# Weight sums for the seven-product down units: built in device memory by copying and adding DMAs

## The chip, the cores and the metric

The kernel runs on one core of a Trainium2 chip. The metric is the device time of one execution in microseconds. All arithmetic on the data is float32, and a matrix product is made of three products of split operands (a rounded part "hi" and a remainder "lo", in a reduced float32 form that TensorE takes).

## The reference

A two-layer decoder trunk on a sequence of 512 tokens, width 1024. Each layer has a token mixer (attention heads), an MLP with a squared ReLU, and a gated embedding:

```python
for i in range(DEPTH):                                   # DEPTH = 2
    hn = rmsnorm(h, norm_mix_g[i])
    h = h + mixer(hn, ...)                               # even: stick-breaking + differential; odd: dilated
    hn = rmsnorm(h, norm_mlp_g[i])
    u = jnp.square(jax.nn.relu(hn @ w_mlp_up[i]))        # 1024 -> 4096
    h = h + u @ w_mlp_down[i]                            # 4096 -> 1024
    gate = jax.nn.sigmoid(rmsnorm(h, norm_ple_g[i]) @ w_ple_gate[i])
    h = h + (p[i] @ w_ple_proj[i]) * gate
return rmsnorm(h, final_norm_g)
```

The change concerns `u @ w_mlp_down[i]` alone.

## The kernel before, in words

The layers run one after the other: mixer, MLP, gated embedding. Weights lie in device memory, packed into blocks of 1 MiB ([128 partitions, 2048 columns]). `wload` fetches one block into a tile called `raw`, of which there are two buffers; `wsplit` makes `wh` (ScalarE, line 122) and `wl` (GpSimd, line 126, in two halves, inside the mixers; VectorE, line 128, elsewhere) of half a block at a time, each with three buffers, and TensorE then runs the three products (lines 141, 144, 145). The DMA that loads `raw` (line 114) is issued from SyncE's queue; that queue also carries the attention bias tiles (`bias<-urow`, line 543), the stores of the embedding's projection (`pjd`, line 384) and everything else that is a plain copy. DMAs that add into their target are issued from GpSimd's queue, where the `wl` subtractions of the mixers also stand. Each queue is worked in order: a DMA or an instruction that waits holds back what stands behind it on the same queue. The order in which each engine's instructions stand is made by a scheduling layer when the kernel is built. It may put an instruction ahead of ones written earlier in the code, as long as what it depends on is kept. A DMA is told finished through one of eight semaphores that the queue's DMAs use in turn, so at most eight from SyncE's queue are under way.

The MLP runs in four chunks of 1024 hidden columns. `up(ch, c)` makes a quarter of a chunk's hidden values; `down(ch, c)` multiplies a chunk by one of four column groups of the down weights. A `down` unit is a 2 by 2 block product done with seven block products instead of eight (a Winograd scheme): its 1 MiB block of weights holds four quarters A12, A22, A21, A11, and besides the quarters it needs four sums of them,

- S1 = A21 + A22 and S3 = A21 + A11 (tile `s13`),
- S2 = S1 + A11 and S4 = S2 + A12 (tile `s24`).

In chunks 0 to 2 VectorE makes the four sums with four additions of [128, 512] (lines 799, 800, 801, 804). In chunk 3 `s13` is made by two loading DMAs on SyncE's queue (line 783) and one adding DMA on GpSimd's (line 784), and VectorE makes only `s24`. The sixteenth unit of a layer (chunk 3, group 3) is computed in the plain way and needs no sums. So 15 units in each of two layers use sums. `split` (line 813 on ScalarE, 814 on VectorE) then makes the hi and lo tiles.

Of the kernel before, what the change touches and what calls it, by code (L numbers as in the profile page):

```python
# [12 lines left out]
F32 = mybir.dt.float32  # L13
# [3 lines left out]
ALU = mybir.AluOpType  # L17
AX = mybir.AxisListType

P = 128  # L20
D = 1024
S = 512
# [5 lines left out]
DEPTH = 2  # L28
# [34 lines left out]
def trunk(  # L63
# [5 lines left out]
    nc = tc.nc  # L69
    uid = [0]  # L70

    def nm(s):
        uid[0] += 1
        return f"{s}_{uid[0]}"

    cpool = ctx.enter_context(tc.tile_pool(name="cpool", bufs=1))
    dpool = ctx.enter_context(tc.tile_pool(name="dpool", bufs=1, space=bass.MemoryType.DRAM))
# [26 lines left out]
    def ps_wide():  # L104
        t = ps(wide[wide_i[0] % 8])
        wide_i[0] += 1
        return t
# [4 lines left out]
    def wload(src):  # L112
        raw = wpool.tile([P, src.shape[-1]], F32, tag="raw", name=nm("raw"), bufs=2)
        nc.sync.dma_start(raw, src)
        return raw

    def wsplit(raw, i, nk, n, pool=None):
        bufs = 3 if pool is None else 4
        hi = (pool or wpool).tile([P, nk, n], F32R, tag="wh", name=nm("wh"), bufs=bufs)
        lo = (pool or wpool).tile([P, nk, n], F32R, tag="wl", name=nm("wl"), bufs=bufs)  # L120
        src = raw[:, i * nk * n:(i + 1) * nk * n].rearrange("p (k c) -> p k c", k=nk)
        act = nc.scalar.activation(hi, src, AF.Copy)  # L122
        if lo_eng[0] is nc.gpsimd:
            for x in range(2):
                kx = slice(x * nk // 2, (x + 1) * nk // 2)
                nc.gpsimd.tensor_tensor(lo[:, kx], src[:, kx], hi[:, kx].bitcast(F32), op=ALU.subtract)  # L126
        else:
            last_low[:] = [nc.vector.tensor_tensor(lo, src, hi.bitcast(F32), op=ALU.subtract).ins]  # L128
        last_high[:] = [act.ins]
        return hi, lo  # L130
# [3 lines left out]
    def block(src, nk, n):  # L134
        raw = wload(src)
        return [wsplit(raw, i, nk, n) for i in range(src.shape[-1] // (nk * n))]
# [15 lines left out]
    def lin_units(accs, ws, ahl, k0, nk, outer):  # L152
        pairs = [(i, k) for k in range(nk) for i in range(len(accs))] if outer else \
            [(i, k) for i in range(len(accs)) for k in range(nk)]
        for i, k in pairs:
            ah, al = ahl[k0 + k]
            mm3(accs[i], ws[i][0][:, k], ws[i][1][:, k], ah, al, k == 0, k == nk - 1)
            yield 2.0

    def run(units):  # L160
        for _ in units:
            pass
# [62 lines left out]
    def use_tables(after):  # L225
        ins = nc.scalar.preload_act_table_set("natural_log_exp_and_others").ins
        for a in after:
            order(ins, a)
        return ins

    def order(later, earlier):
        tc.add_manual_dep(
            later, earlier.name,
            mybir.DependencyInfo(mybir.DependencyClass.NoSync, mybir.DependencyReason.DATA),
            reason="activation tables")
# [498 lines left out]
    def mlp(layer, fpool, norm, nxt):  # L734
# [4 lines left out]
        hidden, spare, stages, b12, low, lows, high = {}, [], [], [], [], [], []  # L739

        def up(ch, c):
            blk = block(w_up[layer, 4 * ch + c], KT, P)
            accs = [ps_wide() for _ in range(2)]
            run(lin_units(accs, blk, ahl, 0, KT, ch == 0 and c == 0))
            if not rstd:
                rstd.append(norm.finish(use_tables(sig_tail) if layer == 0 else None))
            u = fpool.tile([P, 7, HW], F32, tag="u", name=nm("u"), bufs=1)
            if ch == NCH - 1:
                if c == 0:
                    b12.append((fpool.tile([P, HW], F32R, tag="b12", name=nm("b12"), bufs=1), masks))  # L750
                else:
                    if c == 1:
                        spare.append(fpool.tile([P, 7, HW], F32R, tag="uh", name=nm("spare"), bufs=5))
                        stages.append(fpool.tile([P, 7 * HW], F32, tag="ul", name=nm("stage"), bufs=5))
                        add_up(stages[0][:, 0:2 * S].rearrange("p (s c) -> p s c", s=2), w_down[layer, 4 * ch + 1])
                    b12.append((spare[0][:, 2 * c - 2], spare[0][:, 2 * c - 1]))
            uh = fpool.tile([P, 7, HW], F32R, tag="uh", name=nm("uh"), bufs=5)
            ul = fpool.tile([P, 7, HW], F32R, tag="ul", name=nm("ul"), bufs=5)
            chain = []
            for i, acc in enumerate(accs):  # L760
                ui = u[:, B11 + 2 * i:B11 + 2 * i + 2].rearrange("p a c -> p (a c)")
                chain.append(nc.vector.scalar_tensor_tensor(ui, acc, 0.0, rstd[0], op0=ALU.max, op1=ALU.mult).ins)  # L762
                chain.append(nc.scalar.activation(ui, ui, AF.Square, scale=0.5).ins)  # L763
            if ch == NCH - 1:
                hi, lo = b12[c]
                nc.scalar.activation(hi, u[:, T3], AF.Copy)
                nc.vector.tensor_tensor(lo, u[:, T3], hi.bitcast(F32), op=ALU.subtract)
            nc.vector.tensor_tensor(
                u[:, T1:T3 + 1:2], u[:, B11:B22 + 1:3], u[:, T3:T3 + 1].to_broadcast([P, 2, HW]), op=ALU.subtract)
            nc.vector.scalar_tensor_tensor(  # L770
                u[:, T2], u[:, T1], -1.0, u[:, B22], op0=ALU.mult, op1=ALU.subtract)
            t4 = nc.vector.scalar_tensor_tensor(  # L772
                u[:, T4], u[:, T2], -1.0, u[:, B21], op0=ALU.mult, op1=ALU.subtract)
            nc.scalar.activation(uh, u, AF.Copy)  # L774
            part = nc.vector.tensor_tensor(ul, u, uh.bitcast(F32), op=ALU.subtract)  # L775
            hidden[ch, c] = (uh, ul, part.ins, chain[0], chain[3], t4.ins)

        A12, A22, A21, A11 = range(4)

        def add_up(s13, src):  # L780
            sv = src.rearrange("p (s c) -> p s c", s=4)
            for x in range(2):
                nc.sync.dma_start(s13[:, x], sv[:, A21])
            nc.gpsimd.dma_start(s13, sv[:, A22:A11 + 1:2], accum_op=ALU.add)  # L784

        def down(ch, c):
            src = w_down[layer, 4 * ch + c]
            raw = wload(src)
            rv = raw.rearrange("p (s k c) -> p s (k c)", s=4, k=4)
            last = ch == NCH - 1  # L790
            if last and c == 1:
                s13 = stages[0][:, 0:2 * S].rearrange("p (s c) -> p s c", s=2)
            else:
                s13 = fpool.tile([P, 2, S], F32, tag="s13", name=nm("s13"), bufs=1)
            s24 = fpool.tile([P, 2, S], F32, tag="s24", name=nm("s24"), bufs=1)
            if last and c != 1:
                add_up(s13, src)
            elif not last:
                nc.vector.tensor_tensor(s13[:, 0], rv[:, A21], rv[:, A22], op=ALU.add)
                nc.vector.tensor_tensor(s13[:, 1], rv[:, A21], rv[:, A11], op=ALU.add)  # L800
            sum2 = nc.vector.tensor_tensor(s24[:, 0], s13[:, 0], rv[:, A11], op=ALU.add).ins
            if last and c:
                order(sum2, hidden[ch, 3][2] if c == 1 else lows[-1])
            nc.vector.tensor_tensor(s24[:, 1], s24[:, 0], rv[:, A12], op=ALU.add)

            def split(src):
                n = src.shape[1]
# [24 lines left out]
            if last:  # L832
                stage = [stages[0] if c == 1 else fpool.tile([P, 7 * HW], F32, tag="u", name=nm("u"), bufs=1), 0]
# [96 lines left out]
        for c in range(4):  # L930
            up(0, c)
        for ch in range(1, NCH):
            up(ch, 0)
            for c in range(4):
                down(ch - 1, c)
            for c in range(1, 4):
                up(ch, c)
        side_sums(3)
        for c in range(3):
            down(NCH - 1, c)  # L940
# [152 lines left out]
def _pack4(w, r0, c0):  # L1093

    t = w[r0 * P:(r0 + 8) * P, c0:c0 + 2 * P].reshape(4, 2, P, 2, P)
    return np.stack([t[:, j, :, i].transpose(1, 0, 2) for i, j in ((0, 1), (1, 1), (1, 0), (0, 0))], axis=1).reshape(P, -1)


def _feeds(a):
# [64 lines left out]
```

## Time and profile before

| | |
|---|---|
| median of 3 runs | 1294.68 us (1294.04 to 1295.32) |
| profiled execution: first to last instruction | 1293.1 us, 1.6 us under the median |
| TensorE busy | 1275.4 us |
| VectorE busy | 1003.9 us |
| GpSimd busy | 212.9 us |
| moved by the DMA queues | 144.25 MB, mean 112 GB/s |

The profiled execution's own time is known by its span; the runs' median lies 1.6 us above it, which is taken as what lies around the span. The mixer of layer 0 ends at about 262 us, its MLP at about 610 us; the mixer of layer 1 runs from about 650 to 900 us, its MLP to about 1230 us. The page lists for each engine its busy time and for each group of instructions the idle time ahead of it with what ended it. A busy share for TensorE near one says that it hardly ever waits, and a wait of another engine costs nothing by itself.

### The profile page before, as it was taken

Reading aid. Unit: us, or ns where it says so; the run is one execution under the profiler, and the core shown is the slowest. Engines: PE = TensorE matmul, PEld = TensorE weight load, DVE = VectorE, ACT = ScalarE, POOL = GpSimd, SP = SyncE. Lnnn points to the kernel's source line nnn. Section 1 sums busy time; section 2 is a strip of 40 time slices with the busy share of each in tenths; the row PEclk is TensorE's granted clock in tenths of the full one; section 3 lists DMA queues with packets and bytes.
Section 4 is the critical chain, followed back from the end, with each engine's and each line's share of the span. In section 5 each row is a group of like instructions: output and inputs, shape, how many; then the busy total and the mean of one; then the engine's idle time right before and its main releaser. Section 6 shows DMA issues by size and latency. Waiting matters only on the chain.

```text
span 1293.1 us, 19313 instructions
## 1 busy us (share of the span) xinstructions
PE 1275.4 (99%) x7520; PEld 1124.2 (87%) x7520; DVE 1003.9 (78%) x1666; ACT 709.5 (55%) x1146; POOL 212.9 (16%) x184
## 2 busy tenths in 40 slices
PE   9999999999999999999999999999999999999996
PEld 7988887888988989989889888788899898898986
DVE  6788798778848869779767777887785795986976
ACT  6667868555535335356456666765554443534544
POOL 2433434400000000001024333222000000000201
PEclk9999999999999999999999999999999999999999
DMA  6321423222222222638432222212323223255751
GB/s 211 144 82 54 159 75 114 90 98 98 95 102 98 98 98 98 195 107 219 140 127 86 82 90 75 73 58 80 116 98 101 95 99 115 82 148 146 173 178 66
DMA packets 33995, 144.25 MB, mean 112 GB/s; under 512 B 3888, under 2 KB 4624, under 8 KB 21232
## 3 DMA queue, kind: packets, MB, share of 16 engines
q1 hardware_dynamic: 29680, 135.16, 30.9%
q0 software_dynamic: 4224, 7.87, 3.6%
q8 instruction: 59, 0.97, 0.3%
q14 instruction: 32, 0.26, 0.1%
HBM read 131.92 MB, written 6.37 MB: 107 GB/s over the span
## 4 chain that ended last, share of the span: by engine, by line
PE 87%; DVE 7%; ACT 3%; issue 1%; DMA 0%; SPq 0%; POOL 0%; DVEq 0%; ACTq 0%; POOLq 0%
PE mm L141 11%; PE mm L144 11%; PE mm L145 11%; PE sc L144 6%; PE sc L145 6%; PE sc L141 5%; PE pv L145 5%; PE pv L144 5%; PE pv L141 5%; PE tp L145 4%; PE tp L144 4%; PE tp L141 4%; PE pv L581 3%; PE tp L560 2%; PE tp L900 2%
## 5 line engine op out<-in xcount | busy, mean ns | idle before, releaser
L122 ACT ACTIVATE wh<-raw 128x1024 fp32r<-128x1024 f32 (+1 forms) x156 | 160.5, 1034 | 142.6 <-PE mm L144 54.5
L126 POOL TENSOR_TENSOR wl<-raw,wh 128x512 fp32r<-128x512 f32 (+1 forms) x132 | 178.2, 1372 | 303.4 <-ACT wh L122 303.4
L141 PE MATMUL mm<-hi,wh 128*128 128x512 f32 x472 | 187.1, 396 | 0.6 <-DVE tmp L495 0.4
L145 PE MATMUL mm<-hi,wl 128*128 128x512 f32 x472 | 184.8, 391 | 0.1
L144 PE MATMUL mm<-lo,wh 128*128 128x512 f32 x472 | 184.6, 391 | 0.0
L128 DVE TENSOR_TENSOR wl<-raw,wh 128x1024 fp32r<-128x1024 f32 x90 | 109.5, 1223 | 39.6 <-ACT wh L122 34.1
L145 PEld LDWEIGHTS mm<-hi,wl 128*128 128x128 f32 x472 | 88.6, 188 | 20.0 <-POOL wl L126 0.5
L141 PEld LDWEIGHTS mm<-hi,wh 128*128 128x128 f32 x472 | 88.7, 188 | 17.5 <-DVE tmp L495 0.8
L144 PEld LDWEIGHTS mm<-lo,wh 128*128 128x128 f32 x472 | 88.8, 188 | 15.5
L784 POOL DMA_DIRECT2D s<-in_w_down_dram x4 | 4.5, 1123 | 578.7 <-DMA s<-in_w_down_dram 312.9
L813 ACT ACTIVATE wh<-s 128x1024 fp32r<-128x1024 f32 x58 | 61.1, 1054 | 54.5 <-DVE s L800 14.7
L554 ACT ACTIVATE e<-e,mn 128x128 f32<-128x128 f32 (+3 forms) x96 | 53.8, 561 | 62.5 <-DVE mn L551 62.2
L775 DVE TENSOR_TENSOR ul<-u,uh 128x1792 fp32r<-128x1792 f32 x32 | 64.8, 2024 | 29.4 <-ACT uh L774 29.2
L814 DVE TENSOR_TENSOR wl<-s,wh 128x1024 fp32r<-128x1024 f32 x58 | 70.9, 1222 | 16.6 <-ACT wh L813 16.3
L774 ACT ACTIVATE uh<-u 128x1792 fp32r<-128x1792 f32 x32 | 54.5, 1702 | 45.9 <-DVE u L772 45.9
L763 ACT ACTIVATE u<-u 128x512 f32<-128x512 f32 x64 | 39.7, 626 | 68.1 <-DVE u L762 68.1
L144 PE MATMUL sc<-lo,wh 128*128 128x512 f32 x184 | 72.0, 392 | 0.8 <-DVE lo L188 0.6
L141 PE MATMUL sc<-hi,wh 128*128 128x512 f32 x184 | 71.9, 391 | 0.7 <-ACT hi L187 0.7
L145 PE MATMUL sc<-hi,wl 128*128 128x512 f32 x184 | 71.8, 390 | 0.0
L141 PE MATMUL mm<-wh,hi 128*128 128x256 f32 (+1 forms) x216 | 63.3, 293 | 0.0
L145 PE MATMUL mm<-wh,lo 128*128 128x256 f32 (+1 forms) x216 | 63.0, 292 | 0.0
L144 PE MATMUL mm<-wl,hi 128*128 128x256 f32 (+1 forms) x216 | 62.9, 291 | 0.0
(308 smaller groups left out, 3884.5 us busy)
## 6 DMA issues: line engine op xcount, KB each, us to landing
raw<-in_w_up_dram SPq DMA_DIRECT2D x32, 1024.0 KB, 4.9
raw<-in_w_down_dram SPq DMA_DIRECT2D x32, 1024.0 KB, 4.9
raw<-in_w_in_dram SPq DMA_DIRECT2D x23, 1024.0 KB, 4.9
raw<-in_w_gate_dram SPq DMA_DIRECT2D x8, 1024.0 KB, 4.9
bias<-urow SPq DMA_DIRECT2D x24, 256.0 KB, 3.6
raw<-in_w_outa_dram SPq DMA_DIRECT2D x8, 768.0 KB, 4.2
pj<-pjd SPq DMA_DIRECT2D x16, 256.0 KB, 4.8
h<-in_xT_dram SPq DMA_DIRECT2D x8, 256.0 KB, 5.8
```

The costliest lines, as they stand in the source:

```text
L122: act = nc.scalar.activation(hi, src, AF.Copy)
L126: nc.gpsimd.tensor_tensor(lo[:, kx], src[:, kx], hi[:, kx].bitcast(F32), op=ALU.subtract)
L128: last_low[:] = [nc.vector.tensor_tensor(lo, src, hi.bitcast(F32), op=ALU.subtract).ins]
L141: mm = nc.tensor.matmul(acc, lh, rh, start=start, stop=False)
L144: nc.tensor.matmul(acc, lh, rl, start=False, stop=False)
L145: return mm.ins, nc.tensor.matmul(acc, ll, rh, start=False, stop=stop).ins
L554: nc.scalar.activation(e[:, 0:n], e[:, 0:n], AF.Exp, scale=-1.0, bias=mn, accum_out=s)
L763: chain.append(nc.scalar.activation(ui, ui, AF.Square, scale=0.5).ins)
L774: nc.scalar.activation(uh, u, AF.Copy)
L775: part = nc.vector.tensor_tensor(ul, u, uh.bitcast(F32), op=ALU.subtract)
L813: high[:] = [nc.scalar.activation(hi, src, AF.Copy).ins]
L814: low[:] = [nc.vector.tensor_tensor(lo, src, hi.bitcast(F32), op=ALU.subtract).ins]
```

## The change

The four sums of all 30 units are no longer made where they are used. For each unit there is now a buffer of four quarters (1 MiB) in device memory, and seven DMAs build the sums there:

1. two copies of A21 from the weights, into S1 and S3 (SyncE's queue, line 132);
2. one adding DMA of A22 and A11 together onto S1 and S3 (GpSimd's queue, line 135);
3. a copy of S1 into S2 (SyncE, line 138), then an adding DMA of A11 (GpSimd, line 141);
4. a copy of S2 into S4 (SyncE, line 138), then an adding DMA of A12 (GpSimd, line 141).

Each of these waits for the one before it of the same unit. They are written as a generator whose steps are taken one at each `wload` from the fourth on; at step n, unit n begins, unit n-1 takes its second stage, and so on, with six stages. `down` then loads A12, A22, A11 (768 KiB instead of 1 MiB) and the two tiles `s13` and `s24` (512 KiB each) with DMAs on SyncE's queue (lines 818, 819). VectorE's additions, and the separate path of chunk 3, are gone. The order of the quarters in the packed weights changes so that A22 and A11 lie side by side and A21 last.

```diff
     def wload(src):
         raw = wpool.tile([P, src.shape[-1]], F32, tag="raw", name=nm("raw"), bufs=2)
         nc.sync.dma_start(raw, src)
+        if nload[0] >= 3:
+            next(ticks, None)
+        nload[0] += 1
         return raw
+    nload = [0]
+    A12, A22, A11, A21 = range(4)
+    S1, S3, S2, S4 = range(4)
+    sums = {(layer, ch, c): dpool.tile([P, 4, S], F32, ...)
+            for layer in range(DEPTH) for ch in range(4) for c in range(4) if (ch, c) != (3, 3)}
+    def weight_sums():
+        def quarter(u, x, n=1):
+            return w_down[u[0], 4 * u[1] + u[2]].rearrange("p (s c) -> p s c", s=4)[:, x:x + n]
+        def begin(u):
+            for x in (S1, S3):
+                nc.sync.dma_start(sums[u][:, x:x + 1], quarter(u, A21))
+        def both(u):
+            nc.gpsimd.dma_start(sums[u][:, S1:S3 + 1], quarter(u, A22, 2), accum_op=ALU.add)
+        def copy(dst, src):
+            return lambda u: nc.sync.dma_start(sums[u][:, dst:dst + 1], sums[u][:, src:src + 1])
+        def add(dst, x):
+            return lambda u: nc.gpsimd.dma_start(sums[u][:, dst:dst + 1], quarter(u, x), accum_op=ALU.add)
+        stages = (begin, both, copy(S2, S1), add(S2, A11), copy(S4, S2), add(S4, A12))
+        units = list(sums)
+        for n in range(len(units) + len(stages) - 1):
+            for m, stage in reversed(list(enumerate(stages))):
+                if 0 <= n - m < len(units):
+                    stage(units[n - m])
+            yield
+    ticks = weight_sums()
...
         def down(ch, c):
-            src = w_down[layer, 4 * ch + c]
-            raw = wload(src)
-            rv = raw.rearrange("p (s k c) -> p s (k c)", s=4, k=4)
+            raw = wload(w_down[layer, 4 * ch + c, :, 0:3 * S])
+            rv = raw.rearrange("p (s c) -> p s c", s=3)
             last = ch == NCH - 1
...
-                nc.vector.tensor_tensor(s13[:, 0], rv[:, A21], rv[:, A22], op=ALU.add)
-                nc.vector.tensor_tensor(s13[:, 1], rv[:, A21], rv[:, A11], op=ALU.add)
-            sum2 = nc.vector.tensor_tensor(s24[:, 0], s13[:, 0], rv[:, A11], op=ALU.add).ins
...
-            nc.vector.tensor_tensor(s24[:, 1], s24[:, 0], rv[:, A12], op=ALU.add)
+            s13, s24 = (fpool.tile([P, 2, S], F32, tag=t, name=nm(t), bufs=1) for t in ("s13", "s24"))
+            nc.sync.dma_start(s13, sums[layer, ch, c][:, S1:S3 + 1])
+            nc.sync.dma_start(s24, sums[layer, ch, c][:, S2:S4 + 1])
```

How this moves the queues is seen in the order in which the instructions stand. On SyncE's queue, in the mixer of layer 0, between the loads of two neighbouring weight blocks (`raw_145` and `raw_191`; the first number of a tile is the same in both kernels where it is the same block), there stood only four bias tiles:

```order
L114 DMA raw_145_776<-in_w_in_dram 128x2048
L543 DMA bias_97_582<-urow_177 128x512
L543 DMA bias_98_584<-urow_177 128x512
L543 DMA bias_135_747<-urow_177 128x512
L543 DMA bias_136_749<-urow_177 128x512
L114 DMA raw_191_959<-in_w_in_dram 128x2048
```

Now the same stretch and the one after it read as follows (`sums002` is the buffer of layer 0, chunk 0, group 2; a row `sums<-in_w_down_dram` is a beginning copy, `sums<-sums` a later one):

```order
L114 DMA raw_145_806<-in_w_in_dram 128x2048
L132 DMA sums002_74<-in_w_down_dram 128x512
L138 DMA sums001_73<-sums001_73 128x512
L132 DMA sums003_75<-in_w_down_dram 128x512 x2
L138 DMA sums000_72<-sums000_72 128x512
L132 DMA sums010_76<-in_w_down_dram 128x512 x2
L132 DMA sums011_77<-in_w_down_dram 128x512
L114 DMA raw_191_991<-in_w_in_dram 128x2048
L138 DMA sums002_74<-sums002_74 128x512
L138 DMA sums001_73<-sums001_73 128x512
L138 DMA sums003_75<-sums003_75 128x512
```

Nine or so copying DMAs stand between neighbouring weight loads; those of line 138 wait for an adding DMA of GpSimd's queue. On that queue, in the same place, the subtractions for `wl` followed each other:

```order
L126 TENSOR_TENSOR wl_147_779<-raw_145_776,wh_146_778 128x512 x2
L126 TENSOR_TENSOR wl_149_784<-raw_145_776,wh_148_783 128x512 x2
L126 TENSOR_TENSOR wl_193_962<-raw_191_959,wh_192_961 128x512 x2
L126 TENSOR_TENSOR wl_195_967<-raw_191_959,wh_194_966 128x512 x2
L126 TENSOR_TENSOR wl_218_1094<-raw_214_1089,wh_217_1093 128x512 x2
```

and now adding DMAs stand between them:

```order
L162 TENSOR_TENSOR wl_147_811<-raw_145_806,wh_146_810 128x512 x2
L141 DMA sums002_74<-in_w_down_dram 128x512
L141 DMA sums001_73<-in_w_down_dram 128x512
L141 DMA sums003_75<-in_w_down_dram 128x512
L135 DMA sums011_77<-in_w_down_dram 128x1024
L141 DMA sums010_76<-in_w_down_dram 128x512
L135 DMA sums012_78<-in_w_down_dram 128x1024
L162 TENSOR_TENSOR wl_149_816<-raw_145_806,wh_148_815 128x512 x2
```

Each adding DMA waits for a copy on SyncE's queue, and the second `wl` stands behind six of them. The steps that the code takes at later loads are moved ahead: the last of the 120 building DMAs on SyncE's queue, that of layer 1's unit `sums132`, stands between two loads of the mixer of layer 0:

```order
L404 DMA raw_461_2376<-in_pT_dram 128x2x512
L138 DMA sums130_99<-sums130_99 128x512
L138 DMA sums132_101<-sums132_101 128x512
L138 DMA sums131_100<-sums131_100 128x512
L138 DMA sums132_101<-sums132_101 128x512
L114 DMA raw_464_2383<-in_w_proj_dram 128x2048
```

where these two loads followed each other before:

```order
L368 DMA raw_461_2298<-in_pT_dram 128x2x512
L114 DMA raw_464_2305<-in_w_proj_dram 128x2048
```

So the sums of both layers are built during the first part of the mixer of layer 0, and twelve weight loads of that mixer stand among the copies.

More of the change, by code (lines that the diff above doesn't have):

```diff
@@ L114, in wload @@
         nc.sync.dma_start(raw, src)
-        return raw
+        if nload[0] >= 3:
+            next(ticks, None)
+        nload[0] += 1
+        return raw
+    nload = [0]
+    A12, A22, A11, A21 = range(4)
+    S1, S3, S2, S4 = range(4)
+    sums = {(layer, ch, c): dpool.tile([P, 4, S], F32, tag=f"sums{layer}{ch}{c}", name=f"sums{layer}{ch}{c}")
+            for layer in range(DEPTH) for ch in range(4) for c in range(4) if (ch, c) != (3, 3)}
[19 more added lines that the diff above has]
+    ticks = weight_sums()
     def wsplit(raw, i, nk, n, pool=None):
@@ L754, in up @@
                         stages.append(fpool.tile([P, 7 * HW], F32, tag="ul", name=nm("stage"), bufs=5))
-                        add_up(stages[0][:, 0:2 * S].rearrange("p (s c) -> p s c", s=2), w_down[layer, 4 * ch + 1])
                     b12.append((spare[0][:, 2 * c - 2], spare[0][:, 2 * c - 1]))
@@ L776, in up @@
             hidden[ch, c] = (uh, ul, part.ins, chain[0], chain[3], t4.ins)
[L778 to L784, printed above, removed]
         def down(ch, c):
-            src = w_down[layer, 4 * ch + c]
-            raw = wload(src)
-            rv = raw.rearrange("p (s k c) -> p s (k c)", s=4, k=4)
+            raw = wload(w_down[layer, 4 * ch + c, :, 0:3 * S])
+            rv = raw.rearrange("p (s c) -> p s c", s=3)
             last = ch == NCH - 1
[L791 to L804, printed above, removed]
+            s13, s24 = (fpool.tile([P, 2, S], F32, tag=t, name=nm(t), bufs=1) for t in ("s13", "s24"))
+            nc.sync.dma_start(s13, sums[layer, ch, c][:, S1:S3 + 1])
+            nc.sync.dma_start(s24, sums[layer, ch, c][:, S2:S4 + 1])
             def split(src):
@@ L1095, in _pack4 @@
     t = w[r0 * P:(r0 + 8) * P, c0:c0 + 2 * P].reshape(4, 2, P, 2, P)
-    return np.stack([t[:, j, :, i].transpose(1, 0, 2) for i, j in ((0, 1), (1, 1), (1, 0), (0, 0))], axis=1).reshape(P, -1)
+    return np.stack([t[:, j, :, i].transpose(1, 0, 2) for i, j in ((0, 1), (1, 1), (0, 0), (1, 0))], axis=1).reshape(P, -1)
 def _feeds(a):
```

## The prediction, made before the changed kernel was run

> **What bounds the kernel now.** I read the page's head, the waits of TensorE, and then its busy time stage by stage.
>
> ```profile
> span 1293.1 us, 19313 instructions
> PE 1275.4 (99%) x7520; PEld 1124.2 (87%) x7520; DVE 1003.9 (78%) x1666; ACT 709.5 (55%) x1146; POOL 212.9 (16%) x184
> ```
>
> TensorE (PE) is idle for 1293.1 - 1275.4 = 17.7 us in all. The windows (length, then busy time of each engine, the granted clock, the mean share of the 16 DMA engines, GB/s) say where it is not:
>
> ```profile
> 15.00:165.00 150.00, 148.91 (x886) 129.96 (x885) 124.56 (x240) 105.74 (x217) 60.28 (x42) 1.00 0.34 112
> 262.00:345.00 83.00, 83.00 (x432) 71.47 (x431) 70.26 (x92) 46.26 (x58) 0.29 (x1) 1.00 0.28 98
> 345.00:520.00 175.00, 175.00 (x1123) 159.97 (x1122) 131.22 (x166) 74.07 (x81) 0.00 (x0) 1.00 0.29 99
> 520.00:610.00 90.00, 89.96 (x603) 83.00 (x602) 71.53 (x109) 44.57 (x56) 11.21 (x12) 1.00 0.64 172
> 900.00:1170.00 270.00, 270.00 (x1669) 244.08 (x1668) 206.74 (x265) 118.84 (x132) 2.19 (x2) 1.00 0.33 109
> ```
>
> In both MLPs (262 to 610, 900 to 1170) TensorE is busy all the time; in the part of the first mixer that matters here it lacks 1.1 of 150 us. So the kernel's time is TensorE's work, and a change moves the time only by taking TensorE's work away (this one doesn't) or by making TensorE wait.
>
> **The change part by part.** *Removed: VectorE's additions.*
>
> ```profile
> L804 DVE TENSOR_TENSOR s<-s,raw 128x512 f32<-128x512 f32 x30 | 20.6, 687 | 0.3
> L801 DVE TENSOR_TENSOR s<-s,raw 128x512 f32<-128x512 f32 x28 | 19.2, 684 | 1.4 <-issue 1.0 <-DMA raw<-in_w_down_dram 0.5
> L799 DVE TENSOR_TENSOR s<-raw 128x512 f32<-128x512 f32 x24 | 16.5, 687 | 2.7 <-DMA raw<-in_w_down_dram 2.4
> L800 DVE TENSOR_TENSOR s<-raw 128x512 f32<-128x512 f32 x24 | 16.4, 684 | 0.0
> ```
>
> 30 + 28 + 24 + 24, and two more that read `stage`, are 108 additions of 0.685 us, 74 us of VectorE. TensorE's work lies over all of it: in the MLP windows above it has 0.04 us of idle time. Worth at most that, so 0.
>
> *Added in the MLPs: loads.* Per unit 256 KiB less of `raw` and 1 MiB more of sums, 0.79 MB net, 23.6 MB over both MLPs. With the rate worked out below (2.96 us per MB) this is 70 us of DMA time in windows whose DMA share is 0.28 to 0.33 (0.64 in the last chunk, which loses its own building DMAs). `s13` and `s24` are asked for when the unit before has split its own, a whole unit ahead of use, and land in about 5 us: 0 on the path; 0 to 3 us if the first pair, which waits for memory of the mixer, holds back the second `w_up` block.
>
> *Added in the mixer of layer 0: the building.* Per unit 1 MiB of copies (four of 256 KiB, SyncE's queue) and 1 MiB of adding (512 + 256 + 256 KiB, GpSimd's queue); 30 units make 31.5 MB of each. The trace of before has no DMA from device memory to device memory, and the price is bounded by the two kinds that it has (queue, kind: packets, MB, share of 16 engines' span):
>
> ```profile
> q1 hardware_dynamic: 29680, 135.16, 30.9%
> q0 software_dynamic: 4224, 7.87, 3.6%
> ```
>
> Plain: 0.309 x 1293.1 / 135.16 = 2.96 us of all 16 engines per MB. Adding: 0.036 x 1293.1 / 7.87 = 5.91 us per MB, twice as much, as an adding DMA also reads its target. So:
>
> - copies 31.5 x 2.96 = 93 us. Bounds: 93 (the other side in SBUF, as in the rows), and 186, if reading and writing the same memory cost two passes.
> - adding 31.5 x 5.91 = 186 us. Bounds: 93, if the doubling belonged to SBUF targets, and 279, three passes at 2.96.
>
> I take the rows themselves, 93 + 186 = 279 us, since each transfer there does the same reads and writes with one side elsewhere; the bounds are 186 and 465.
>
> A page of the Trainium skill, DMA: Bandwidth & Descriptors, section Latency and other measured facts, speaks against the cheap copy: it measured copies between tensors in device memory at 207 to 214 GB/s in each direction. That would be 4.7 us per MB, 147 us instead of 93, and the sum below would come out 54 us higher. No run so far shows it.
>
> What is there to hide 279 us? The order has the first copies behind the third weight load, and the last ahead of the load of `w_proj`:
>
> ```profile
> 17.55 7.91 SPq L114 DMA_DIRECT2D raw<-in_w_in_dram  x2
> ...
> 155.65 0.34 SPq L114 DMA_DIRECT2D raw<-in_w_in_dram  x1
> ...
> 163.45 0.38 SPq L368 DMA_DIRECT2D raw<-in_pT_dram  x1
> 179.45 0.33 SPq L114 DMA_DIRECT2D raw<-in_w_proj_dram  x1
> ```
>
> From 17.55 to 163.45 are 146 us, at a share of 0.34 (the first window): 96 us of free DMA time. The queue is worked in order, so a weight load can't overtake the copies ahead of it, and those wait for adding DMAs; TensorE gets the blocks at the pace of the building. What doesn't fit is 279 - 96 = **183 us**.
>
> Two smaller terms stand against each other. A load is asked for ahead of need:
>
> ```profile
> 170.15 2.55 POOL L126 TENSOR_TENSOR wl<-raw,wh 128x512 fp32r<-128x512 f32 x2 [6.73 <-ACT wh L122]
> ```
>
> The block asked for at 155.65 is subtracted at 170.15; less its landing (4.9, below) and ScalarE's copy (1.05) some 8.6 us of delay are taken up. And the engines aren't filled while the first unit runs its first two links (4.0 + 7.1, rows below). I let them cancel.
>
> *The instructions that issue.* GpSimd issues 90 adding DMAs:
>
> ```profile
> L784 POOL DMA_DIRECT2D s<-in_w_down_dram x4: 1079/1091/1232, 527.9 to 1190.5; - x4
> L839 POOL DMA_DIRECT2D side<-stage x4: 847/856/858, 584.4 to 1209.8; - x4
> ```
>
> 30 x 1.09 + 60 x 0.86 = 84 us, beside 60.3 us of `wl` work in the 150 us window: 144 of 150 unstretched, far less in a stretch that lasts 330. What counts on GpSimd is not the issuing but the waiting: each `wl` stands behind adding DMAs that wait for copies, so `wl` is late by the same delay, not by another. SyncE's 120 issues at 0.33 us are 40 us, nothing.
>
> Sum: the profiled execution's 1293.1 + 183 = 1476, and the 1.6 us between span and median: **1478 us**.
>
> **The rivals.**
>
> *Device memory pays twice.* Copies at two passes (186) with adding as measured: 372 - 96 = +276, 1571 us; with adding at three passes 465 - 96 = +369, 1664. For it: both sides of these transfers are in the same memory, at rates near what a load reaches. Against: no row. With the page's copy rate it would be +237, 1532.
>
> *The links set the pace, not the bytes.* If copies and adding ran side by side at half the price or less, a unit's chain of seven transfers would count:
>
> ```profile
> s<-in_w_down_dram SPq DMA_DIRECT2D x8, 256.0 KB, 4.0
> pjd<-tmp SPq DMA_DIRECT2D x8, 256.0 KB, 3.9
> s<-in_w_down_dram POOLq DMA_DIRECT2D x4, 512.0 KB, 7.1
> side<-u POOLq DMA_DIRECT2D x8, 256.0 KB, 4.5
> raw<-in_w_in_dram SPq DMA_DIRECT2D x23, 1024.0 KB, 4.9
> ```
>
> 4.0 + 7.1 + 3.9 + 4.5 + 3.9 + 4.5 = 27.9 us, six units in flight, 4.7 us a unit; 30 x 4.7 + 27.9 = 168 us where 146 are there: +22, **1317 us**. Between this and my sum lies adding at the plain price: 186 - 96 = +90, 1385. Against: 7.1 us for 512 KiB against 4.9 for 1 MiB says that adding costs bytes.
>
> *Hidden, and not slower.* The DMA engines are two thirds idle, and the first sums are needed only when the MLP starts; if the building fits into the gaps, TensorE waits for nothing and the time stays 1294 to 1295, with VectorE's 74 us as room that nobody uses. The point from which this decides: 63 MB in 96 + 9 us of free time, 1.7 us per MB over both kinds, against 2.96 and 5.91 in the rows. The same would follow if the building stood behind the loads or were spread to the MLPs; the order says that it doesn't.
>
> **How the numbers follow.** My sum (1420 to 1530): 0.48. Device memory twice (1530 to 1665): 0.30. Links, or cheap adding (1300 to 1420): 0.12. Hidden: 0.04. Beyond all these, stalls of the two queues on each other that add to the bytes: 0.06. The range from 1390 to 1630 leaves out the hidden case, most of the links case and the upper end of the memory case, about 0.2. A measurement of this kernel tells 0.2%, 2.6 us, from no change. Faster has 0.015 (TensorE's few waits for VectorE outside the MLPs), the same 0.03, slower the rest, 0.955.
>
> **What would show it.** Right: TensorE idle for about 180 us, nearly all between 30 and 340 us, before `wh` and `wl`; GpSimd waiting for DMAs into `sums`; DMA share over 0.85 in that stretch; q0 at about 36 MB and still 5.9 us per MB, q1 at 187 MB and still 3.0; the MLPs as long as before (348 us from 262 to 610) with VectorE at 930 us busy. The memory rival shows as over 4 us per MB on q1 in that stretch, the links rival as a DMA share well under 0.8 there. Wrong would be a TensorE without gaps in the mixer, or gaps in the MLPs.

## The result and the profile after

The changed kernel takes 1541.68 us (median of 4 runs, 1536.52 to 1544.74) where the kernel before takes 1294.87 beside it: a ratio of 1.19, interval 1.1886 to 1.1915, slower by 247 us. The forecast was 1478 us in a range of 1390 to 1630.

The head of the page after, with TensorE's line and the two DMA queues (packets, MB, share of 16 engines' span):

```profile
span 1542.9 us, 19699 instructions
PE 1319.3 (86%) x7520; PEld 1155.7 (75%) x7520; DVE 932.9 (60%) x1558; ACT 712.0 (46%) x1146; POOL 272.1 (18%) x268
...
q1 hardware_dynamic: 53872, 187.07, 37.9%
q0 software_dynamic: 15552, 36.18, 16.0%
```

VectorE lost 71 us of work, nearly the 74 that were counted, and gained nothing for it. TensorE is now idle for 1542.9 - 1319.3 = 224 us, where it was idle for 17.7; the other 44 us of the 250 by which the span grew are longer busy time of the same 7520 matmuls. Where it waits is read first from SyncE's order. This is the timeline of SyncE's queue after (start, length, line, transfer):

```profile
16.66 0.35 SPq L114 DMA_DIRECT2D raw<-in_w_in_dram  x1
17.05 2.60 SPq L132 DMA_DIRECT2D sums<-in_w_down_dram  x4
24.81 0.34 SPq L114 DMA_DIRECT2D raw<-in_w_in_dram  x1
...
49.08 0.48 SPq L138 DMA_DIRECT2D sums<-sums  x1
49.60 2.53 SPq L132 DMA_DIRECT2D sums<-in_w_down_dram  x3
54.05 0.34 SPq L114 DMA_DIRECT2D raw<-in_w_in_dram  x1
61.42 10.76 SPq L138 DMA_DIRECT2D sums<-sums  x3
...
431.65 0.33 SPq L114 DMA_DIRECT2D raw<-in_w_proj_dram  x1
...
499.99 0.33 SPq L114 DMA_DIRECT2D raw<-in_w_up_dram  x1
```

and this the one row of before that the prediction did not show, the first load of the first MLP:

```profile
252.02 0.33 SPq L114 DMA_DIRECT2D raw<-in_w_up_dram  x1
```

The weight loads stand between copies, and the load of `w_proj` behind the last of them comes at 431.65 instead of 179.45, 252 us later. The MLP starts 248 us later (499.99 instead of 252.02) and the end is 250 us later. So the whole loss arises between 17 and 432 us, and the 1041 us from the start of the MLP to the end have become 2 us longer.

The windows (length, busy time of each engine, granted clock, DMA share, GB/s), the waits (total, times, longest), and the two DMA queues from 30 to 420 us alone (packets, MB, share) of the kernel after:

```profile
30.00:420.00 390.00, 190.92 (x937) 161.51 (x935) 125.77 (x254) 112.77 (x231) 120.76 (x128) 0.73 0.97 194
515.00:860.00 345.00, 344.73 (x2138) 311.72 (x2137) 237.88 (x307) 162.93 (x191) 7.91 (x9) 1.00 0.43 138
```

```profile
PE mm L181 <- POOL wl L162: 128.0, 11, 24.5
PE mm L180 <- POOL wl L162: 41.1, 6, 23.8
...
POOL sums L141 <- DMA sums<-sums: 199.9, 38, 13.1
POOL sums L135 <- DMA sums<-in_w_down_dram: 53.5, 11, 11.7
```

```profile
q0 software_dynamic: 12504, 30.60, 54.4%
q1 hardware_dynamic: 20704, 44.84, 42.8%
```

From 30 to 420 us TensorE works for 191 of 390 us. It waits for GpSimd's `wl` (128.0 + 41.1 us), and GpSimd waits for the copies (199.9 + 53.5 us). The DMA share is 0.97, at 194 GB/s. The MLP has no gap (344.73 of 345), at a DMA share of 0.43. In outline this is the picture of the forecast. What doesn't fit is the size: 252 us instead of 183.

### The profile page after: what moved, and what is told of

Its sections match the earlier page's. It is cut to its first block, busy times and chain, and to the rows that moved or that the text cites. A ratio compares the mean times of both kernels' runs of the same rounds, so it can differ in the third digit from the quotient of the medians.

```text
span 1542.9 us, 19699 instructions
## 1 busy us (share of the span) xinstructions
PE 1319.3 (86%) x7520; PEld 1155.7 (75%) x7520; DVE 932.9 (60%) x1558; ACT 712.0 (46%) x1146; POOL 272.1 (18%) x268
## 3 DMA queue, kind: packets, MB, share of 16 engines
q0 software_dynamic: 15552, 36.18, 16.0%
## 4 chain that ended last, share of the span: by engine, by line
PE 63%; DMA 25%; DVE 6%; issue 2%; ACT 1%; POOL 1%; SPq 1%; DVEq 0%; POOLq 0%; ACTq 0%
DMA sums<-in_w_down_dram 15%; DMA sums<-sums 8%; PE mm L177 7%; PE mm L180 7%; PE mm L181 7%; PE sc L180 4%; PE sc L181 4%; PE sc L177 4%; PE pv L181 4%; PE pv L180 4%; PE pv L177 4%; PE tp L181 3%; PE tp L180 3%; PE tp L177 3%; PE pv L617 2%
## 5 line engine op out<-in xcount | busy, mean ns | idle before, releaser
L181 PE MATMUL mm<-hi,wl 128*128 128x512 f32 x472 | 194.4, 412 | 101.0 <-POOL wl L162 100.9
L177 PE MATMUL mm<-hi,wh 128*128 128x512 f32 x472 | 193.7, 410 | 0.6 <-DVE tmp L531 0.4
L180 PE MATMUL mm<-lo,wh 128*128 128x512 f32 x472 | 190.9, 405 | 0.0
L181 PEld LDWEIGHTS mm<-hi,wl 128*128 128x128 f32 x472 | 93.3, 198 | 125.8 <-POOL wl L162 105.3
L854 POOL DMA_DIRECT2D side<-u x8 | 7.8, 1214 | 632.9 <-ACT u L853 632.9
L605 DVE TENSOR_TENSOR ptl<-tp,pth 128x128 fp32r<-128x128 f32 (+1 forms) x112 | 54.3, 486 | 60.6 <-ACT pth L604 60.4
L141 POOL DMA_DIRECT2D sums<-in_w_down_dram x60 | 52.1, 892 | 218.5 <-DMA sums<-sums 199.9
L587 DVE CUSTOM_DVE_ANT_0 e<-sc,bias 128x128 f32<-128x128 f32 (+3 forms) x96 | 46.1, 484 | 73.2 <-PE sc L571 72.5
L180 PEld LDWEIGHTS mm<-wl,hi 128*128 128x128 f32 x216 | 44.3, 205 | 42.5 <-POOL wl L162 41.9
L604 ACT ACTIVATE pth<-tp 128x128 fp32r<-128x128 f32 (+1 forms) x112 | 47.8, 429 | 55.2 <-PE tp L596 54.6
## 6 DMA issues: line engine op xcount, KB each, us to landing
sums<-in_w_down_dram SPq DMA_DIRECT2D x60, 256.0 KB, 11.2
```

The costliest lines, as they stand in the source:

```text
L177: mm = nc.tensor.matmul(acc, lh, rh, start=start, stop=False)
L180: nc.tensor.matmul(acc, lh, rl, start=False, stop=False)
L181: return mm.ins, nc.tensor.matmul(acc, ll, rh, start=False, stop=stop).ins
L605: evicts[:] = [a.ins, nc.vector.tensor_tensor(dl, src, dh.bitcast(F32), op=ALU.subtract).ins]
```

## The experiments

### What the transfers cost by themselves

Not a piece of the kernel but seven plain loops of 32 steps: a step is one transfer of 256 KiB, or in the last two loops one on each queue, and a barrier stands behind each loop. It computes nothing of the reference. Behind a first loop of loads into SBUF come these six:

```
for j in range(N): sync:   there[j] <- weights           # copy in device memory
for j in range(N): gpsimd: plain[j] <- weights           # the same from GpSimd's queue
for j in range(N): gpsimd: here[j]  += weights           # adding, target in SBUF
for j in range(N): gpsimd: there[j] += weights           # adding, target in device memory
for j in range(N): sync: also[j] <- weights; gpsimd: there[j] += weights
for j in range(N): sync: also2[j] <- there[j]; gpsimd: here[j] += weights
```

> A kernel of its own that computes nothing of the trunk: seven stretches, a barrier of all engines between them, each of 32 transfers of 256 KiB (8.4 MB) with no waits but that at most eight of a queue are under way: loads into SBUF; copies from device memory to device memory from SyncE's queue; the same from GpSimd's queue; adding into SBUF; adding into device memory; copies and adding in device memory side by side; copies in device memory beside adding into SBUF. By the prices of the prediction (2.96 us per MB plain, 5.91 adding, whichever memory): 25, 25, 25 to 30 (bound by issuing), 50, 50, 75, 75 us, each and 3 to 4 us of latency. If device memory pays twice (the rival): copies 39 us at 214 GB/s, adding into device memory over 60, the two side by side over 99 us, while the two stretches that end in SBUF stay at 25 and 50. If the links set the pace (the other rival): as in the first case or quicker, 75 us or less side by side.

Windows inside the stretches, in the order of the loops with the loads into SBUF first (length, GpSimd's busy time, clock, DMA share, GB/s), and the page's rate in 40 slices:

```profile
3.00:20.00 17.00, 0.00 (x0) 1.00 1.00 358
30.00:50.00 20.00, 0.00 (x0) 1.00 1.00 304
60.00:80.00 20.00, 12.50 (x25) 1.00 0.97 301
92.00:122.00 30.00, 22.48 (x27) 1.00 1.11 196
137.00:172.00 35.00, 23.63 (x29) 1.00 1.09 190
185.00:235.00 50.00, 20.47 (x26) 1.00 1.11 247
258.00:305.00 47.00, 22.27 (x26) 1.00 1.08 255
...
GB/s 223 384 380 161 312 316 213 262 317 308 149 178 205 205 204 162 118 204 203 203 205 113 219 244 256 259 258 260 261 178 117 263 253 261 261 262 259 254 99 214
```

Copies inside device memory run at 304 to 317 GB/s, 3.2 us per MB. Adding runs at 203 to 205 GB/s where the stretch is even, 4.9 us per MB, whether its target is in SBUF or in device memory. Both kinds side by side take nearly the sum of their prices: equal bytes at 3.2 and 4.9 make 4.05 us per MB, 247 GB/s; the windows have 247 and 255, and the even slices 253 to 263. So device memory does not pay twice, and the two queues share one budget of DMA time. The Trainium skill (DMA: Bandwidth & Descriptors, Latency and other measured facts) has 207 to 214 GB/s in each direction for copies in rows of 16 KiB at large row pitches; the copies here, in rows of 2 KiB, ran faster than that. The building is worth 31.5 x 3.2 + 31.5 x 4.9 = **255 us** of DMA time, less than the 279 that were forecast; at the 260 GB/s of the even slices it would be 242, so 255 is rather high than low.

With this price the forecast's own sum would be 255 - 96 = 159 us. The load of `w_proj` is 252 late. 93 us are missing, and the next four runs look for them. In their expectations the *bytes theory* says that the delay goes with the bytes that are moved, the *links theory* that it goes with the number of transfers that wait for one another (a link is one transfer of such a chain). For each run the stretch from the first copy to the load of `w_proj` is split into the bytes of the building at these prices, the stretch's own loads (0.34 of the time that it had before, 55 us, or 51 where it begins later), and the rest. For the changed kernel the rest is 105 us and not 93, as the stretch reaches 16 us further here than in the forecast (179.45 against 163.45).

### Copying where the kernel adds

```diff
-            nc.gpsimd.dma_start(sums[u][:, S1:S3 + 1], quarter(u, A22, 2), accum_op=ALU.add)
+            nc.gpsimd.dma_start(sums[u][:, S1:S3 + 1], quarter(u, A22, 2))
-            return lambda u: nc.gpsimd.dma_start(sums[u][:, dst:dst + 1], quarter(u, x), accum_op=ALU.add)
+            return lambda u: nc.gpsimd.dma_start(sums[u][:, dst:dst + 1], quarter(u, x))
```

> The three adding DMAs of a unit copy instead of adding, from the same queue, with the same bytes, order and waits; the sums are therefore not formed. The building took 1541.7 - 1294.9 = 247 us over the 96 us of free time, 343 us. Bytes theory: the adding half of the bytes falls to the plain price, two thirds remain, 229 us, so +133, about 1428. Links theory: the chain of seven and its waits are the same and only some landings get shorter: +200 or more, 1495 and up. Device memory pays twice: all 63 MB at 4.67 us per MB are 294 us, so +198, about 1493.

1455.55 us, and in its timeline of SyncE's queue:

```profile
344.13 0.33 SPq L114 DMA_DIRECT2D raw<-in_w_proj_dram  x1
```

The same chains with cheaper bytes save 86 us, less than the 114 of the bytes theory and more than the 47 that the links theory allows at most. Bytes count, but not they alone: the stretch of 327 us holds 63 x 3.2 = 202 us of building and 55 of loads, which leaves 70.

### The building of half the rows

```diff
-            return w_down[u[0], 4 * u[1] + u[2]].rearrange("p (s c) -> p s c", s=4)[:, x:x + n]
+            return w_down[u[0], 4 * u[1] + u[2]].rearrange("p (s c) -> p s c", s=4)[0:64, x:x + n]
```

All seven DMAs of each unit take 64 of 128 rows (their targets too), and the units load quarters of the weights in the place of the sums, so the sums of this run are not used.

> The building's DMAs take 64 of 128 rows: as many DMAs, in the same order with the same waits, and half the bytes, in packets of the same size. The units load quarters of the weights in place of the sums, so that their sums are not used. Bytes theory, wherever the price lies: 343 / 2 = 171 us less the 96 free, +75, about 1370, or some 9 us less by the lead of the loads. Links theory: the links stay, each landing loses its share of bytes: +180 or more, 1475 and up.

1373.05 us, where the bytes theory had 1370 and the links theory 1475 or more. Window and load:

```profile
20.00:300.00 280.00, 224.65 (x1172) 190.73 (x1171) 189.32 (x309) 146.72 (x297) 147.19 (x148) 0.88 0.80 192
...
260.09 0.33 SPq L114 DMA_DIRECT2D raw<-in_w_proj_dram  x1
```

Half the bytes take away 169 of 247 us with the number of links unchanged. The rest is 60 us here (242 - 127 - 55). It shrinks with the bytes too, so it is no fixed price per link: a link lasts as long as its transfer, and the beginning copies landed in 5.3 us in the median where the full ones took 11.2.

### No link, the same transfers

Each of the seven DMAs has a target of its own, copies plainly, and reads the weights, so none waits for another of its unit. The units load quarters of the weights. The counterpart, with the chains kept, is the run that copies where the kernel adds.

```diff
-            nc.gpsimd.dma_start(sums[u][:, S1:S3 + 1], quarter(u, A22, 2), accum_op=ALU.add)
+            nc.gpsimd.dma_start(sums[u][:, 2:4], quarter(u, A22, 2))
-            return lambda u: nc.sync.dma_start(sums[u][:, dst:dst + 1], sums[u][:, src:src + 1])
+            return lambda u: nc.sync.dma_start(sums[u][:, 2 + dst:3 + dst], quarter(u, src))
-            return lambda u: nc.gpsimd.dma_start(sums[u][:, dst:dst + 1], quarter(u, x), accum_op=ALU.add)
+            return lambda u: nc.gpsimd.dma_start(sums[u][:, 4 + dst:5 + dst], quarter(u, x))
```

> As plain_for_adding (1455.6), with the same number of DMAs, bytes, queues and nearly the same order, but each of the seven writes a place of its own and reads the weights, so none waits for another of its unit; the units load quarters of the weights, no sums are formed. The lone stretches gave 3.2 us per MB for copies in device memory: 63 MB are 201 us, the kernel's own transfers to the load of w_proj 49, so that load is issued at 17.5 + 250 = 268 us instead of 344. If the engines stood unfilled because of the links: +88, about 1383, or 9 less by the lead. If the unfilled part comes from elsewhere (the 1 MiB loads and their buffers, packets slowed in the mixture): it stays near 1455.

1422.22 us, 33 less than with links. The window of this kernel, its load of `w_proj`, and SyncE's wait ahead of the later copies:

```profile
20.00:300.00 280.00, 182.31 (x948) 154.14 (x947) 138.05 (x257) 115.35 (x234) 99.71 (x122) 0.81 0.95 282
...
305.12 0.34 SPq L114 DMA_DIRECT2D raw<-in_w_proj_dram  x1
...
SPq L138 <- DMA sums<-in_w_down_dram: 48.2, 29, 4.3
```

and the same window and wait of its counterpart with links:

```profile
20.00:300.00 280.00, 162.33 (x790) 136.34 (x789) 104.05 (x227) 97.10 (x196) 87.25 (x114) 0.77 0.94 251
...
SPq L138 <- DMA sums<-in_w_down_dram: 180.1, 50, 12.6
```

Without links 282 GB/s pass instead of 251, at nearly the same DMA share (0.95 and 0.94), and SyncE waits 48 us instead of 180 ahead of the later copies. The first copy of this kernel comes 13 us later (30.1 instead of 17.2), and the rest of its stretch is 275 - 202 - 51 = 22 us instead of 70. The time stands halfway between the two numbers expected; the later start takes part of the gain back. By the rest of the stretch the links carry 48 of 70 us, by the time of the kernel 33.

### One DMA for two units

Two units share each DMA: 16 chains instead of 30, the same bytes, all sums made.

```diff
-        units = list(sums)
+        units = groups_of      # (layer, first unit, 2), the last of a layer alone
-            return lambda u: nc.sync.dma_start(sums[u][:, dst:dst + 1], sums[u][:, src:src + 1])
+            return lambda u: nc.sync.dma_start(built[u][:, :, dst:dst + 1], built[u][:, :, src:src + 1])
```

> The whole change with its sums, but one DMA serves two neighbouring units: 16 chains of seven instead of 30, the same bytes in packets of the same size. Prices of the lone stretches: 31.5 MB copied at 3.2 and 31.5 added at 4.9 us per MB, 255 us, and 49 of the kernel's own, 304 of the 414 us that passed; 110 us unfilled. If these go with the number of links, half are left: about 1487. If they go with the bytes: 1541 as before.

1477.2 us, 64 less, and 10 less than the 1487 that the links theory made of it, with this load of `w_proj`:

```profile
365.34 0.33 SPq L114 DMA_DIRECT2D raw<-in_w_proj_dram  x1
```

| kernel | time | stretch | building at 3.2 and 4.9 | own loads | rest |
|---|---|---|---|---|---|
| as changed | 1541.7 | 415 | 255 | 55 | 105 |
| copying for adding | 1455.6 | 327 | 202 | 55 | 70 |
| the same without links | 1422.2 | 275 | 202 | 51 | 22 |
| half the rows | 1373.1 | 242 | 127 | 55 | 60 |
| one DMA for two units | 1477.2 | 348 | 255 | 55 | 38 |

So about two thirds of the rest go when the same bytes stand in half as many, larger DMAs (105 to 38), and about two thirds go when the chains are cut (70 to 22, with plain copies; in the adding kernel the chains were not cut). Larger DMAs change two things at once, the number of links and the size of a transfer. The remaining 20 to 40 us are not explained. These four are single runs, like that of the plain loops; the differences of 33 to 170 us are far over the spread of the runs (8 us for the kernel after).

### No building at all

```diff
-    ticks = weight_sums()
+    ticks = iter(())
-            nc.sync.dma_start(s13, sums[layer, ch, c][:, S1:S3 + 1])
-            nc.sync.dma_start(s24, sums[layer, ch, c][:, S2:S4 + 1])
+            four = w_down[layer, 4 * ch + c].rearrange("p (s c) -> p s c", s=4)
+            nc.sync.dma_start(s13, four[:, S1:S3 + 1])
+            nc.sync.dma_start(s24, four[:, S2:S4 + 1])
```

> No sums are built; s13 and s24 are loaded, with the same bytes, from quarters of the weights themselves, so the sums are wrong. This is the part of the change in the MLPs alone: 108 additions of VectorE less, 23.6 MB of loads more. All theories put the delay in the building, so 1294 to 1298: the prediction gave 0 to VectorE's 74 us and 0 to 3 us to the loads; the changed kernel's trace lost 1.8 us behind the mixer of layer 0. If VectorE's relief were worth something the time would fall under 1292.

1296.8 us (11 runs), ratio 1.0011, interval 1.0002 to 1.002. This is the rest of the change by itself: the additions gone, the larger loads in (quarters of the weights in the place of the sums, the same bytes). Together they cost 1.4 us. As TensorE had 0.04 us of idle time in the MLP windows before, VectorE's relief had nothing to give there, and the 23.6 MB of loads are all but hidden.

### The building spread over loads

The copies are ordered behind a weight load, and a step of the building is taken at every second load. All sums are made.

```diff
-        nc.sync.dma_start(raw, src)
-        if nload[0] >= 3:
+        load[0] = nc.sync.dma_start(raw, src).ins
+        if nload[0] >= 3 and nload[0] % 2:
             next(ticks, None)
...
+        def behind(dma):
+            order(dma.ins, load[0])
...
-            return lambda u: nc.sync.dma_start(sums[u][:, dst:dst + 1], sums[u][:, src:src + 1])
+            return lambda u: behind(nc.sync.dma_start(sums[u][:, dst:dst + 1], sums[u][:, src:src + 1]))
```

> The whole change with its sums, but a step of the building is taken at every second weight load, and its copies are held behind that load in SyncE's order, so that the building is spread from the first mixer to the second MLP: one unit in two loads, some 30 us with about a third of the DMA time used, against 8 to 14 us of building. Bytes theory and links theory alike: hidden where it stands, 1295 to 1300, like the kernel without building (1296.8). If the building costs more than the free DMA time of its stretch (contention with the loads wherever it stands): 1310 or more.

1361.29 us (1354.66 to 1364.42), ratio 1.0492, interval 1.0465 to 1.0519. The expectation of a hidden building is wrong. Windows of this kernel:

```profile
20.00:300.00 280.00, 270.31 (x1481) 229.85 (x1480) 225.83 (x380) 181.53 (x359) 114.72 (x93) 0.99 0.62 157
300.00:500.00 200.00, 186.67 (x1122) 166.83 (x1121) 113.68 (x135) 79.83 (x88) 20.69 (x26) 0.98 0.85 213
500.00:700.00 200.00, 183.02 (x1066) 161.09 (x1065) 129.50 (x179) 85.03 (x106) 28.97 (x35) 0.97 0.90 221
```

There is no long gap any more (TensorE's longest wait lasts 5.8 us), but TensorE lacks 10, 13 and 17 us, at DMA shares of 0.62, 0.85 and 0.90, where the kernel without building lacks 2, 0 and 1. Two more runs ask whether it is the fullness or the building as such.

### Each layer's sums in its own mixer

As above, but a step at every load, one generator for each layer, the second started at the end of the first MLP.

```diff
-        if nload[0] >= 3 and nload[0] % 2:
-            next(ticks, None)
+        if nload[0] >= 3:
+            next(ticks[turn[0]], None)
...
+            if last and c == NCH - 1 - 1:
+                turn[0] = min(layer + 1, DEPTH - 1)
```

> Each layer's sums are built in its own mixer, one step of the building behind every weight load, nothing in the MLPs; all sums are correct. By bytes there is just room: a step is 1.05 MB of copies at 3.2 us per MB and 1.05 MB of adding at 4.9, 8.5 us of the engines, and loads stand some 15 us apart in the mixer, of which two thirds, 10 us, are free. If free DMA time is all that counts, the time is 1297 to 1310. If a load that shares the engines comes late even where there is room for both (the run with a step at every second load lost 12 us in the first mixer and 45 between 300 and 820), the share near 0.9 in both mixers costs 20 to 35 us each: 1330 to 1365. By either, TensorE has no gaps in the first MLP after its first units.

1393.15 us (1390.93 to 1396.59), ratio 1.0766, interval 1.0748 to 1.0784: worse than either number. The first mixer, the first MLP without its start, and the second mixer:

```profile
20.00:260.00 240.00, 217.01 (x1211) 186.87 (x1209) 186.85 (x320) 150.06 (x308) 101.94 (x90) 0.95 0.80 189
...
400.00:520.00 120.00, 120.00 (x745) 108.51 (x744) 72.51 (x86) 48.77 (x52) 0.00 (x0) 1.00 0.42 143
...
620.00:820.00 200.00, 174.10 (x964) 150.67 (x962) 131.46 (x229) 99.63 (x169) 60.36 (x69) 0.93 0.97 226
```

Where nothing is built TensorE has no gap; where something is built it has, 23 us at a share of 0.80 and 26 at 0.97.

### Half the building, spread thin

Only layer 1's 15 units are built, a step at every third load from the first mixer to the second; layer 0's units load quarters of the weights.

```diff
-        if nload[0] >= 3 and nload[0] % 2:
+        if nload[0] >= 3 and nload[0] % 3 == 0:
-        units = list(sums)
+        units = [u for u in sums if u[0] == 1]
```

> Only the sums of layer 1 are built (15 units), with a step behind every third weight load from the first mixer on, through the first MLP and into the second mixer; the units of layer 0 load quarters of the weights in the place of their sums, so what is computed in layer 0 is left incomplete. A step of 8.5 us then stands against some 35 us between steps: 0.24 of DMA share more, 0.6 to 0.7 in all. If building that is thin enough is hidden, the time is that of the kernel without building, 1297, up to 1302. If the building delays loads in proportion to its bytes wherever it stands (128 of 255 us of DMA time here, and the run with a step at every second load lost 65 us over all of it), it is 1325 to 1335.

1324.52 us (1321.04 to 1326.77), ratio 1.0224, interval 1.0207 to 1.0242. Even the thin building is not hidden; it costs 28 us over the kernel without building, almost the number of the theory that the delay goes with the bytes (1325 to 1335). A stretch of the first MLP shows how. First the kernel without building: the window, then from 400 to 620 us ScalarE's wait for the two tiles that hold the sums, and their landing time:

```profile
400.00:520.00 120.00, 120.00 (x780) 110.05 (x779) 81.95 (x98) 51.42 (x55) 0.00 (x0) 1.00 0.44 142
...
ACT wh L829 <- DMA s<-in_w_down_dram: 9.0, 3, 3.7
...
s<-in_w_down_dram SPq DMA_DIRECT2D x20, 512.0 KB, 4.5
```

and then with the thin building:

```profile
400.00:520.00 120.00, 110.96 (x646) 98.18 (x645) 68.35 (x82) 44.87 (x49) 7.32 (x9) 0.97 0.63 169
...
ACT wh L832 <- DMA s<-in_w_down_dram: 23.7, 5, 8.7
ACT e L832 <- DMA raw<-in_w_down_dram: 22.1, 7, 7.1
...
s<-in_w_down_dram SPq DMA_DIRECT2D x20, 512.0 KB, 5.3
```

The mean share of 0.63 leaves room. But a unit's loads are asked for only when their buffers come free, a short time ahead of use, and a step of the building is put on the engines at once. A load that meets such a step lands later: between 260 and 620 us the 18 loads of these tiles that were under way beside a building transfer took 7.2 us in the median from the end of their issue, the other 10 took 3.4, and ScalarE's longest wait grows from 3.7 to 8.7 us. It is not the order on SyncE's queue that holds them: between 400 and 620 us that queue waits for buffers that VectorE frees, as in the kernel without building, and no building copy is among the longer waits. TensorE loses 9 us in 120. The mean share does not tell how much: between 260 and 400 us, at 0.76, it loses 2.

What the building cost in each kernel, over the 1296.8 us without it, per us of DMA time that it needs: 245 of 255 as changed, 96 of 255 by layer, 64 of 255 at every second load, 28 of 128 spread thin. It falls from 0.96 to 0.22 with spreading, and did not reach zero in any run. Not all of it is waiting. TensorE's own busy time grows too, for the same 7520 matmuls: without building, spread thin, at every second load and by layer it reads

```profile
PE 1276.3 (98%) x7520; PEld 1124.7 (87%) x7520; DVE 941.1 (73%) x1558; ACT 709.5 (55%) x1146; POOL 206.3 (16%) x178
PE 1286.1 (97%) x7520; PEld 1129.6 (85%) x7520; DVE 943.4 (71%) x1558; ACT 709.1 (54%) x1146; POOL 241.8 (18%) x223
PE 1296.8 (95%) x7520; PEld 1134.5 (83%) x7520; DVE 954.0 (70%) x1558; ACT 708.5 (52%) x1146; POOL 276.4 (20%) x268
PE 1305.1 (94%) x7520; PEld 1142.6 (82%) x7520; DVE 975.2 (70%) x1558; ACT 709.7 (51%) x1146; POOL 267.2 (19%) x268
```

at mean granted clocks of 0.997, 0.994, 0.986 and 0.972. So of the 28, 64 and 96 us about 10, 20 and 29 are longer work beside a lower clock, and the rest is idle time.

## Why the prediction was right or wrong

**What bounds the kernel: right.** VectorE's 74 us were worth nothing. The run without building has their loss and the larger loads together, and is not faster (1296.8); the first MLP of the changed kernel has no gap.

**The loads in the MLPs: right.** 0 to 3 us were forecast for the first pair; the run without building is 1.4 us over the kernel before.

**Where and by which mechanism: right in the main.** The loss stands in the first mixer alone. SyncE's loads are held by copies, GpSimd's `wl` stands behind adding DMAs that wait for copies, and TensorE has 199 us without work between 30 and 420 (180 were forecast between 30 and 340). The DMA share is 0.97 (over 0.85 was forecast).

**The price of the bytes: near.** 279 us were forecast and 255 measured. Copies came at 3.2 us per MB (2.96 forecast), adding at 4.9 (5.91), and adding is not dearer in device memory. The row of before was packet time divided by bytes, and packet times overlap: the same division on the lone adding loop gives 1.11 / 0.196 = 5.7 us per MB (share over MB per us) where 4.9 passed. So q0 "still 5.9 us per MB" was no sign of the price either; it came at 0.160 x 1542.9 / 36.18 = 6.8.

**The step that failed: "I let them cancel".** The forecast took the DMA engines as filled from the first copy to the last, and let the unfilled engines at the start stand against the loads' lead of 8.6 us. The engines moved too few bytes all through the stretch (184 to 199 GB/s in four pieces between 30 and 420 us, where the loops with both kinds side by side passed 247 and 255), not only at its start: 252 us of delay against the 159 that the measured prices make, 93 us where the forecast had none. The runs show what most of it is: cutting the chains takes 48 of 70 us away (33 by the time of the kernel), halving the number of DMAs 67 of 105. So the chain of seven dependent transfers did count, on top of the bytes and not, as the rival on links had it, in their place. With the price 24 us too high and this term 93 too low, the delay came out 69 us under the measured one, and the time 64. That the two errors partly cancel is luck: with the measured price the same sum would have said 1454. And 1541.7 lies above the 1420 to 1530 that the forecast gave to its own sum; it is inside the range by the room that was left for device memory paying twice, which is not there.

**"DMA share well under 0.8" as the sign of links: wrong.** The share was 0.97 in the changed kernel, and in the copying one 0.94 with the chains and 0.95 without them, while the rate went from 251 to 282 GB/s. In the mixture the packets themselves are longer: from 30 to 420 us a plain one of 2 KB lasts 84 ns in the median but 129 ns in the mean (107 in the lone copies), and an adding one 178 and 250 (183 and 185 in the mean of the lone adding loops). The share counts this as busy. So the row that was to tell the rivals apart could not.

**The rivals.** *Device memory pays twice* gave 1532 to 1571, which holds the measured time, by a mechanism that isn't there: copies at 304 to 317 GB/s, adding at one price for both memories, and q1 in the stretch at 0.428 x 390 / 44.84 = 3.7 us per MB, not over 4 (nor at the 3.0 of the forecast, as its packets are longer there; 3.1 over the whole kernel). A time that fits is no evidence for a cause. *Links alone* gave 1317, and half the rows with all links came at 1373 and not at 1475 or more. *Hidden* fell, and one sentence with it: that the same would follow if the building stood behind the loads or were spread to the MLPs. It was tried three times and cost 96, 64 and 28 us. The case with 0.06, stalls of the two queues on each other that add to the bytes, comes nearest to the mechanism, though its 93 us stayed inside the range.

**What stays open.** 20 to 40 us of the stretch have no cause by these runs, and some 13 more if the building is priced at 260 GB/s. That the queue has at most eight transfers under way may be one cause, and the longer packets of the mixture another; neither was tried alone. How much of the loss comes from TensorE's lower clock was not tried either.

## What to carry to other kernels

Free DMA time is not a budget that can be spent in full: on this kernel, whose busiest engine hardly ever waits and whose loads are asked for shortly before use, each us of added DMA time cost 0.2 us when spread thin and nearly 1 us when packed into one stage. Price such a stage by its bytes, then add what a chain of dependent transfers in in-order queues leaves unfilled: here 105 us on 255 were lost beyond the bytes, of which the chain and the number of transfers account for about two thirds. Fewer and larger transfers won back 67 of these 105. Watch the clock of the busiest engine too. Read the GB/s beside the DMA share: the share was 0.97 at 194 GB/s and 0.95 at 282.

## What the runs showed of the hardware

- Adding DMAs of 256 KiB cost 4.9 us per MB into SBUF and into device memory alike, half as much again as a copy in device memory (3.2).
- The DMA share goes over one (1.11 in a window of adding alone), so the times of packets that it adds up overlap; it is no measure of work done.
- TensorE's granted clock was 0.73 in the stretch where it worked half of the time, and 1.00 in the MLP without gaps; its busy time rose by 44 us (1275.4 to 1319.3). Over five kernels the busy time of the same 7520 matmuls went up as the mean granted clock went down: 1276.3 us at 0.997, 1286.1 at 0.994, 1296.8 at 0.986, 1305.1 at 0.972, 1319.3 at 0.924. No run changed the clock alone.
